# Recurrent branch of a two-layer hybrid block: units of two heads, operands of the next unit beside the chunk chain, modulation moved to attention

## Chip, core and metric

The kernel runs on one core of one Trainium2 chip. The metric is the device time of one execution in microseconds; less is better. TensorE (PE) multiplies, PEld is its loading of weights, VectorE (DVE), ScalarE (ACT) and GpSimd (POOL) do the rest of the arithmetic, and SyncE (SP) issues most of the transfers between memory and the core. All engines run their own instructions in order and wait for each other by semaphores.

## What is computed

Two layers run over 256 latent tokens and 256 context tokens of width 1024. Each layer has an adaptive modulation of the norm, one wide input projection, three branches (latent attention, neighbourhood attention, a recurrent branch), a gated merge and a feed-forward part, which is dense in layer 0 and a mixture of eight experts in layer 1. Layer 1 needs outputs for the latent tokens alone. The parts that this change is about:

```python
mod = (s_lat @ mod_w[l] + mod_b[l])[:, None, :]          # [6 * 1024] per layer, for x and for ctx
h = rms_norm(x, norm1_g[l]) * (1.0 + sc1) + sh1
m_cq, m_ckv, m_kr, n_q, n_k, n_v, r_z, gates = split_last(h @ w_in[l], IN_SIZES)
...
def rwkv_scan(r, w, k, v, kk, a, s0, reverse):
    def step(S, inp):
        r_t, w_t, k_t, v_t, kk_t, a_t = inp
        sa = jnp.einsum('bhij,bhj->bhi', S, -kk_t)
        S = S * w_t[:, :, None, :] + sa[..., None] * (kk_t * a_t)[:, :, None, :] + v_t[..., None] * k_t[:, :, None, :]
        return S, jnp.einsum('bhij,bhj->bhi', S, r_t)
...
x_mid = x + gt1 * merge_branches(ya, yb, yr, gates, mla_wo[l], na_wo[l], rw_wo[l], w_out[l])
```

The scan runs over eight heads of 64, in both directions, first over the context and then over the latents.

## The kernel before

**Stages.** For each layer: norm, recurrent branch, attention start (keys of the latent attention and the operands of the neighbourhood attention), the two attentions with the merge woven in, the output projection, and then the feed-forward part. Only the recurrent branch and the attention are touched here.

**The projection as filler.** `serve` (L451) is a generator that multiplies the normed input with one tile of 128 columns of `w_in` after the other, 57 tiles per layer. A tile is 24 products of 128x512 (three per 128 rows of depth, since each f32 operand is split in two parts whose products make up the f32 result); in layer 1 the tiles that are needed for the latents alone are 256 wide. Its weights come in by SP (512 KB, tile `wraw`, four buffers), ACT makes the upper part `whi` (L469) and POOL the lower part `wlo` (L470). Tiles that the recurrent branch needs stay in SBUF, the others are written to memory (`spill`, L956). `need` (L497) drives the generator until a tile is there.

**Modulation.** `modulation` (L319) is a second generator: a round is eight steps, each of two loads of 512 KB into `wraw` and four products (L339) that fill four strips of one PSUM bank; the next round's result is used only at the end of the layer or in the next one. `serve` takes one such step after each of its tiles (`next(extra, None)`, L492).

**Recurrent branch.** The recurrence is done in chunks of 64 tokens. `rw_half` (L587) treats four heads (two pairs of heads, a pair fills 128 partitions) in both directions. It makes the operands (decays by a scan, L620, exponentials, scaled keys), then the inverse of a 64x64 triangular matrix for each head, direction and chunk: blocks of 16 by substitution on DVE (L701 to L706), merged to 32 and 64 by many 32x32 products (L719, L735, L739, L763 to L772). Then a chain of eight chunks runs (L876 to L908), each of which needs the state `H` of the one before: PE (L882) to ACT (`rs`, L885) to PE (L892) to DVE and ACT (`uv`, L894, L895) to PE (L847) to DVE (`hst`, L850). `rw_front` of the second half runs in the last chunks of the first. `rw_out` (L918) normalizes and stores the result.

**Order of the work.** `weave` (L1634) takes the steps of the recurrent branch in their order; each yields a number of microseconds, and that much of `serve` is put behind it. The order in which instructions then stand on an engine is made from this by the framework's scheduler. PSUM has eight banks: two for the projection (`mm`), one for modulation (`md`), five for the recurrent branch (`rw`).

## Time and profile before

| | us |
|---|---|
| median of three runs | 2992.24 (2989.56 to 2997.04) |
| the profiled execution | 2989.12 |
| its span, first to last instruction | 2987.4 |
| PE busy | 2815.1 (94%), 19774 products |
| PE's weight loads (PEld) busy | 2168.4 (73%) |
| DVE busy | 1901.3 (64%), 2654 instructions |
| ACT busy | 1621.5 (54%), 2449 instructions |
| POOL busy | 369.9 (12%) |

A busy share is an average over stages. Layer 0 takes until about 1260, its recurrent branch 100 to 550; layer 1's recurrent branch lies between 1270 and 1745, and its attention starts there; the experts follow from about 1960. PE counts as busy also where its clock is granted at half rate, so the granted clock is read beside the busy time. The matrix products on small tiles overlap on the engine, so the busy times of their groups add up to more than the time they take.

### The profile page before, as it was taken

The numbers are of one execution on the slowest core, as the hardware profiler recorded it, in microseconds if no ns is written. First come the engines' busy times: TensorE is split into PE (matmuls) and PEld (weight loads), VectorE is DVE, ScalarE is ACT, GpSimd is POOL, SyncE is SP. The second block draws the span as 40 slices with busy tenths as digits, with TensorE's granted clock in tenths as the row PEclk, the third lists the DMA queues.
The fourth block names the chain that finished last, engine by engine and source line by source line (L and its number), as shares of the span: only waits on it lengthen the run. The fifth ranks groups of instructions, "written<-read, shape, count | busy, mean of one in ns | idle before, by whom it ended". The sixth has DMA issues, their size and how long they took to land. (4 is left out here: it accounts for less than half of the span.)

```text
span 2987.4 us, 48726 instructions
## 1 busy us (share of the span) xinstructions
PE 2815.1 (94%) x19774; PEld 2168.4 (73%) x19774; DVE 1901.3 (64%) x2654; ACT 1621.5 (54%) x2449; POOL 369.9 (12%) x287
## 2 busy tenths in 40 slices
PE   7989979999999999997997979989999999999998
PEld 3566667676777888765766856778878787887876
DVE  4653662527754333267347256779988988888897
ACT  3423423447644332253343436667877777777776
POOL 3221221220010000133233400010000000000000
PEclk9989979999999999998997988989999999999999
DMA  7433311441432333343342333669989999998995
GB/s 273 160 130 103 131 57 61 158 143 57 128 127 80 97 99 104 117 143 110 103 149 95 108 104 109 193 239 361 359 320 363 353 350 342 356 361 335 362 352 205
DMA packets 109016, 582.26 MB, mean 195 GB/s; under 512 B 12912, under 2 KB 26608, under 8 KB 86896
## 3 DMA queue, kind: packets, MB, share of 16 engines
q1 hardware_dynamic: 94640, 557.57, 52.1%
q10 hardware_dynamic: 13632, 19.93, 1.8%
q8 instruction: 157, 2.57, 0.4%
q0 software_dynamic: 512, 1.57, 0.1%
q14 instruction: 75, 0.61, 0.1%
HBM read 554.38 MB, written 24.64 MB: 194 GB/s over the span
## 5 line engine op out<-in xcount | busy, mean ns | idle before, releaser
L314 PE MATMUL pmm<-big,whi 128*128 128x512 f32 (+2 forms) x1392 | 534.4, 385 | 11.1 <-ACT stage L958 3.2
L315 PE MATMUL pmm<-big,whi 128*128 128x512 f32 (+2 forms) x1392 | 517.4, 372 | 7.3 <-DVE big L436 3.6
L316 PE MATMUL pmm<-big,wlo 128*128 128x512 f32 (+2 forms) x1392 | 515.9, 371 | 1.9 <-POOL wlo L470 1.9
L1552 DVE TENSOR_TENSOR mwlo<-share,mwhi 128x1024 fp32r<-128x1024 f32 x398 | 472.2, 1229 | 21.0 <-ACT mwhi L1551 11.7
L1551 ACT ACTIVATE mwhi<-share 128x1024 fp32r<-128x1024 f32 x404 | 423.8, 1059 | 94.2 <-PE pmm L316 68.2
L470 POOL TENSOR_TENSOR wlo<-wraw,whi 128x512 fp32r<-128x512 f32 (+1 forms) x228 | 305.0, 1341 | 721.5 <-ACT whi L469 691.9
L315 PE MATMUL pmm<-mwlo,big 128*128 128x512 f32 x896 | 355.1, 396 | 7.2 <-DVE mwlo L1552 6.7
L314 PEld LDWEIGHTS pmm<-big,whi 128*128 128x128 f32 (+1 forms) x1392 | 267.4, 192 | 117.5 <-issue 37.5
L314 PE MATMUL pmm<-mwhi,big 128*128 128x512 f32 x896 | 352.1, 393 | 0.6 <-ACT big L1439 0.6
L316 PE MATMUL pmm<-mwhi,big 128*128 128x512 f32 x896 | 349.8, 390 | 0.0
L299 DVE TENSOR_TENSOR wlo<-wraw,whi 128x512 fp32r<-128x512 f32 x236 | 158.7, 674 | 252.1 <-ACT whi L298 245.6
L1552 DVE TENSOR_TENSOR mwlo<-mraw,mwhi 128x1024 fp32r<-128x1024 f32 x264 | 310.9, 1223 | 9.1 <-ACT mwhi L1551 3.5
L1551 ACT ACTIVATE mwhi<-mraw 128x1024 fp32r<-128x1024 f32 x264 | 278.0, 1060 | 66.8 <-PE pmm L316 49.8
L315 PEld LDWEIGHTS pmm<-big,whi 128*128 128x128 f32 (+1 forms) x1392 | 267.9, 192 | 55.1 <-DVE big L436 6.0
L316 PEld LDWEIGHTS pmm<-big,wlo 128*128 128x128 f32 (+1 forms) x1392 | 268.1, 193 | 50.6 <-issue 5.1
L298 ACT ACTIVATE whi<-wraw 128x512 fp32r<-128x512 f32 x236 | 145.3, 617 | 288.4 <-PE pmm L315 271.9
L469 ACT ACTIVATE whi<-wraw 128x512 fp32r<-128x512 f32 (+1 forms) x228 | 141.8, 624 | 267.4 <-PE pmm L315 228.3
L315 PEld LDWEIGHTS pmm<-mwlo,big 128*128 128x128 f32 x896 | 168.3, 188 | 48.0 <-DVE mwlo L1552 12.3
L314 PEld LDWEIGHTS pmm<-mwhi,big 128*128 128x128 f32 x896 | 168.3, 188 | 36.3 <-ACT big L1439 1.3
L316 PEld LDWEIGHTS pmm<-mwhi,big 128*128 128x128 f32 x896 | 168.3, 188 | 33.4
L315 PE MATMUL pat<-mwlo,mhh 128*128 128x512 f32 x448 | 175.1, 391 | 1.6 <-DVE mwlo L1552 1.4
L314 PE MATMUL pat<-mwhi,mhh 128*128 128x512 f32 x448 | 174.4, 389 | 0.0
(407 smaller groups left out, 4487.0 us busy)
## 6 DMA issues: line engine op xcount, KB each, us to landing
share<-in_moe SPq DMA_DIRECT2D x100, 2048.0 KB, 9.4
mraw<-in_moe SPq DMA_DIRECT2D x66, 2048.0 KB, 9.5
wraw<-in_win SPq DMA_DIRECT2D x112, 512.0 KB, 3.5
wraw<-in_modw SPq DMA_DIRECT2D x80, 512.0 KB, 4.9
wraw<-in_ffn SPq DMA_DIRECT2D x60, 512.0 KB, 3.5
wraw<-in_wo SPq DMA_DIRECT2D x24, 512.0 KB, 3.8
wraw<-in_wout SPq DMA_DIRECT2D x16, 512.0 KB, 4.6
share<-in_modw SPq DMA_DIRECT2D x12, 512.0 KB, 9.0
```

The costliest lines, as they stand in the source:

```text
L298: nc.scalar.activation(hi, raw[:, a:a + b], AF.Copy)
L299: nc.vector.tensor_tensor(lo, raw[:, a:a + b], hi.bitcast(F32), OP.subtract)
L314: nc.tensor.matmul(out, a[0], b[0], start=first, stop=False)
L315: nc.tensor.matmul(out, a[0], b[1], start=False, stop=False)
L316: nc.tensor.matmul(out, a[1], b[0], start=False, stop=last)
L469: nc.scalar.activation(hi, raw[:, k:k + 4], AF.Copy)
L470: nc.gpsimd.tensor_tensor(lo, raw[:, k:k + 4], hi.bitcast(F32), OP.subtract)
L1551: nc.scalar.activation(hi, raw[:, a:a + 2], AF.Copy)
L1552: (nc.gpsimd if a in pool else nc.vector).tensor_tensor(lo, raw[:, a:a + 2], hi.bitcast(F32), OP.subtract)
```

## The change

- **Units of two heads.** `rw_half` becomes `rw_prep` (operands and inverses of one pair of heads) and `rw_chain` (its eight chunks and its output). The chain of pair n runs beside the preparation of pair n+1. The chain has four PSUM banks of its own (`ch`), preparation two (`rw`); each chunk of a pair has half as many products, and copies half as wide.
- **Pacing.** A new function `pace` replaces `weave` there. It keeps a clock for each of the two streams, takes the next step of the one that is behind, adds up an estimate of PE's work, and puts in projection steps while PE's sum is behind the clocks. Steps now yield two numbers, their own time and PE's.
- **Operands.** The scale of the decay and of `kd` moves from DVE to ACT; the backward scan runs on reversed views in place of two corrections; the norm of the keys is made on 128x16 in place of 64x512; the substitution holds two 16-blocks in the partitions' rows as one 16x16 block per item; both `uv` copies are on DVE; `lora` is loaded once.
- **Modulation.** `serve` no longer takes modulation steps. The rounds 1 and 2 of layer 0 and round 0 of layer 1 (24 steps) now alternate with what is left of the projection in layer 0's attention start, the rounds 1 and 2 of layer 1 (16 steps) in layer 1's, and what is left over runs beside the attentions. `router_begin` moves behind them.
- **Rest of the projection.** After the recurrent branch the projection runs until the four `nq` tiles are stored, some of it is woven into the attention start, and all that is left is then done in one piece.

```diff
-    def serve(s, l, t0, extra):
+    def serve(s, l, t0):
...
-            next(extra, None)
             q, q1 = q1, q2
-        for _ in extra:
-            yield 1.0
...
-                V.tensor_scalar(lw, lw, -0.5 * DEC, -0.5 * DEC, op0=OP.mult, op1=OP.add)
-                cum = s.tmp()
-                V.tensor_tensor_scan(cum, s.c("scanm"), lw, 0.0, OP.mult, OP.add)
-                if d:
-                    V.tensor_tensor(lw, lw, cum, OP.subtract)
-                    V.tensor_tensor(c8(lw), c8(lw), c8(cum)[:, :, 63:64].to_broadcast([128, 8, 64]), OP.add)
-                    cum = lw
+            A.activation(lw, lw, AF.Identity, bias=s.m16[:, 98:99], scale=-0.5 * DEC)
...
+            rev = (lambda a: a[:, ::-1]) if d else (lambda a: a)
+            V.tensor_tensor_scan(rev(cum), s.c("scanm"), rev(lw), 0.0, OP.mult, OP.add)
...
+            A.activation(kd, ta, AF.Identity, bias=s.kc1[l][:, hp:hp + 1], scale=s.kc2[l][:, hp:hp + 1])
...
+        for t in range(2, 16):
+            w = pr[:, 0:t * t].rearrange("p (j q) -> p j q", j=t)
+            V.tensor_tensor(w, X[:, t:t + 1, 0:t].to_broadcast([128, t, t]), X[:, 0:t, 0:t].rearrange("p q j -> p j q"), OP.mult)
+            V.tensor_reduce(X[:, t, 0:t], w, AX.X, OP.add)
+            yield 0.4 + t * t / 500.0, 0.0
...
+            yield s.W["chain"], 1.2
+            pu = s.ps(tag="ch")
+            for hh, d in heads:
+                PE.matmul(pu[bp(n, d), col(hh)], TT[HO[d], 8 * hh + ch[d], :], Rs[HO[d], col(hh)], start=(hh == 0), stop=(hh == 1),
+                          skip_group_check=True)
+            for d in range(2):
+                V.tensor_copy(st["uv"][d][bp(n, d)].rearrange("p a b -> p (a b)"), pu[bp(n, d), 0:128])
+            yield s.W["chain"], 0.4
...
+def pace(K, streams, fill):
...
+    while clock:
+        g = min(clock, key=clock.get)
+        w = next(g, None)
...
+        clock[g] += w[0] * K.W["time"]
+        pe += w[1] + K.debt
+        K.debt = 0.0
+        now = min(clock.values())
+        while pe < now:
+            t = next(fill, None)
+            pe += 1e9 if t is None else t
...
         def rwkv(l, t0):
             K.rw_common(l)
...
+            before = []
+            for hp in range(4):
+                K.mark(f"rw{l}{hp}")
+                pace(K, before + [K.rw_prep(l, hp, t0)], K.srv)
+                before = [K.rw_chain(l, hp, t0)]
+            K.mark(f"rw{l}4")
+            pace(K, before, K.srv)
...
-                K.srv = K.serve(l, t0, K.modulation(1, [1, 2]) if l else chain(K.modgen, K.modulation(1, [0])))
-                with K.phase(f"n1{l}", **({} if l else dict(st=1))):
+                K.srv = K.serve(l, t0)
+                mods = K.modulation(1, [1, 2]) if l else chain(K.modgen, K.modulation(1, [0]))
+                with K.phase(f"n1{l}", **({} if l else dict(st=1, md=1))):
...
-                with K.phase(f"rw{l}", rw=5):
...
-                    weave(rwkv(l, t0), K.srv, False)
...
+                with K.phase(f"rw{l}", rw=2, ch=4):
+                    K.W = dict(chain=1.9, time=(1.1, 1.0)[l])
+                    rwkv(l, t0)
+                    while not all((l, f"nq{i}") in K.spilled for i in range(4)):
+                        next(K.srv)
+                with K.phase(f"at{l}", md=1, sc=2, tp=2, py=1):
...
-                    weave(alternate(K.mla_keys(l), K.na_prep(l, t0)), chain(K.srv, mods))
+                    weave(alternate(K.mla_keys(l), K.na_prep(l, t0)), alternate(K.srv, mods), False)
+                    for _ in K.srv:
+                        pass
```

How the order changes on PE inside a chunk of layer 0's first chain. Before, a chunk has the products of four heads (`prw`, L789 scores, L836 and L840 the state), and then projection products (`pmm`):

```order
L789 MATMUL prw_2093<-big_127_719,share_32_289 128x128
L789 MATMUL prw_2094<-big_127_719,share_32_289 128x128
L836 MATMUL prw_2103<-hst_2024,cst 64x256 x2
L840 MATMUL prw_2103<-hst_2024,big_127_719 64x128 x4
L314 MATMUL pmm_2073<-big_30_230,whi_1986 128x512
L315 MATMUL pmm_2073<-big_31_231,whi_1986 128x512
L316 MATMUL pmm_2073<-big_30_230,wlo_1987 128x512
```

In the changed kernel, the second chunk of the first pair. `pch` are products of the chain, L618 and L622 those of the next pair's operands (`prw`), in one order:

```order
L618 MATMUL prw_1331<-zl_337,lora_298 128x512
L867 MATMUL pch_1255<-uv_1205,am_1215 64x64
L867 MATMUL pch_1255<-uv_1206,am_1215 64x64
L867 MATMUL pch_1255<-uv_1205,am_1217 64x64
L867 MATMUL pch_1255<-uv_1206,am_1217 64x64
L622 MATMUL prw_1335<-zl_377,lora_298 128x512
L824 MATMUL pch_1308<-share_34_291,am_1291 64x64 x2
L890 MATMUL pch_1308<-hst_1289,big_42_305 64x128 x2
L803 MATMUL pch_1321<-big_42_305,share_32_289 128x128 x2
L847 MATMUL pch_1326<-hst_1289,cst 64x128 x2
L850 MATMUL pch_1326<-hst_1289,big_42_305 64x128 x2
L900 MATMUL pch_1347<-rs_1318,share_33_290 64x64 x4
```

What moved: where three to six projection products stood between two steps of a chain, products of the next pair's operands now stand, and few projection products. Per layer the three stretches with both streams hold 96, 141 and 96 projection products in layer 0.

SP's queue before, in layer 0's recurrent branch: a projection tile's weights (`in_win`), then one modulation step's two loads (`in_modw`).

```order
L460 DMA wraw_2812<-in_win 128x1024
L334 DMA wraw_2936<-in_modw 128x1024
L334 DMA wraw_2938<-in_modw 128x1024
L460 DMA wraw_2944<-in_win 128x1024
L334 DMA wraw_3053<-in_modw 128x1024
L334 DMA wraw_3055<-in_modw 128x1024
L460 DMA wraw_3061<-in_win 128x1024
```

SP's queue of the changed kernel at the attention start of layer 0:

```order
L334 DMA wraw_5248<-in_modw 128x1024
L334 DMA wraw_5250<-in_modw 128x1024
L334 DMA wraw_5277<-in_modw 128x1024
L334 DMA wraw_5279<-in_modw 128x1024
L334 DMA wraw_5288<-in_modw 128x1024
L334 DMA wraw_5290<-in_modw 128x1024
L460 DMA wraw_5328<-in_win 128x1024
```

What moved: the loads of modulation, one step to a tile before, stand in the attention start eight steps to a tile; 20 of the 24 steps are issued ahead of the piece in which all remaining tiles follow each other.

PE at the same place, the broadcast of the heads' norms (L1139 before, L1142 in the changed kernel). Before:

```order
L1139 MATMUL ptp_5590<-sq_5564,cst 128x512
L1139 MATMUL ptp_5603<-sq_5564,cst 128x512
L315 MATMUL pmm_5576<-big_31_231,whi_5577 128x512
L316 MATMUL pmm_5576<-big_30_230,wlo_5578 128x512
L1139 MATMUL ptp_5609<-sq_5564,cst 128x512
L314 MATMUL pmm_5576<-big_30_230,whi_5577 128x512
L315 MATMUL pmm_5576<-big_31_231,whi_5577 128x512
L316 MATMUL pmm_5576<-big_30_230,wlo_5578 128x512
L1139 MATMUL ptp_5615<-sq_5564,cst 128x512
```

In the changed kernel, with the modulation's products (`pmd`, L339) between them:

```order
L339 MATMUL pmd_5338<-wraw_5370,sT 32x512 x2
L339 MATMUL pmd_5338<-wraw_5372,sT 32x512 x2
L1142 MATMUL ptp_5529<-sq_5481,cst 128x512
L1142 MATMUL ptp_5535<-sq_5481,cst 128x512
L339 MATMUL pmd_5338<-wraw_5381,sT 32x512 x2
L1142 MATMUL ptp_5548<-sq_5481,cst 128x512
L1142 MATMUL ptp_5554<-sq_5481,cst 128x512
L339 MATMUL pmd_5338<-wraw_5383,sT 32x512 x2
L314 MATMUL pmm_5512<-big_30_230,whi_5423 128x512
L1142 MATMUL ptp_5565<-sq_5481,cst 128x512
L339 MATMUL pmd_5338<-wraw_5415,sT 32x512 x2
```

What moved: the attention's own products now stand behind products that wait for a load each. Between the last output of the recurrent branch and the long piece of projection, PE has 126 projection products, 88 of modulation, 48 of the keys' projection (`psc`) and 72 transposes and broadcasts in layer 0; in layer 1 these are 146, 32, 48 and 72.

## Rows read from the trace of the kernel before

**Rows 1.** Busy time by stretch: us, then each engine, granted clock, DMA share, GB/s.
```profile
100.00:220.00 120.00, 107.04 (x1454) 67.46 (x1454) 75.75 (x114) 39.26 (x69) 28.34 (x22) 0.89 0.41 136
220.00:330.00 110.00, 110.00 (x1125) 77.07 (x1118) 36.84 (x63) 38.54 (x78) 20.44 (x16) 1.00 0.35 120
330.00:450.00 120.00, 97.71 (x1446) 72.18 (x1444) 81.90 (x117) 37.39 (x67) 29.74 (x23) 0.83 0.24 82
450.00:540.00 90.00, 90.00 (x954) 67.97 (x954) 25.40 (x43) 33.47 (x68) 18.47 (x14) 1.00 0.26 87
540.00:670.00 130.00, 123.17 (x555) 90.42 (x554) 56.05 (x91) 61.36 (x112) 37.53 (x30) 0.97 0.44 145
1260.00:1430.00 170.00, 146.12 (x1651) 103.84 (x1652) 105.61 (x164) 73.19 (x129) 59.69 (x44) 0.90 0.37 121
1540.00:1650.00 110.00, 87.14 (x1394) 71.83 (x1393) 77.72 (x113) 39.84 (x75) 40.87 (x30) 0.78 0.32 105
1735.00:1825.00 90.00, 70.42 (x297) 43.49 (x293) 55.18 (x119) 40.31 (x78) 1.42 (x3) 0.70 0.24 78
```

**Rows 2.** Waits of PE, 100 to 570: waiter <- releaser: us, times, longest.
```profile
PE prw L662 <- DVE t L660: 16.2, 4, 6.7
...
PE pmd L339 <- DMA wraw<-in_modw: 0.3, 1, 0.3
```

**Rows 3.** Waits of PE, 1260 to 1825.
```profile
PE prw L719 <- DVE share L709: 14.2, 2, 8.7
```

**Rows 4.** Groups of instructions on DVE, 95 to 560: count | busy us, mean ns | idle before.
```profile
L798 DVE TENSOR_TENSOR am<-prw,cst 128x512 f32<-128x512 f32 x32 | 20.7, 685 | 46.4 <-PE prw L789 46.4
L703 DVE TENSOR_TENSOR share<-share 128x8 f32<-128x8 f32 (+13 forms) x28 | 19.7, 704 | 1.0
...
L705 DVE TENSOR_REDUCE share<-share 128x4 f32<-128x8 f32 (+13 forms) x28 | 9.5, 338 | 1.0
...
L894 DVE COPY uv<-prw 64x256 f32<-64x256 f32 x16 | 6.8, 422 | 31.4 <-PE prw L892 29.4 <-ACT whi L469 2.0
...
L622 DVE TENSOR_TENSOR t<-t,t 128x512 f32<-128x512 f32 x4 | 4.6, 1156 | 0.1
L618 DVE TENSOR_SCALAR t<-t 128x512 f32<-128x512 f32 x8 | 4.5, 560 | 7.7 <-ACT t L612 7.7
...
L623 DVE TENSOR_TENSOR t<-t,t 128x512 f32<-128x512 f32 x4 | 3.7, 935 | 0.1
...
L650 DVE TENSOR_SCALAR t<-t,kc,kc 128x512 f32<-128x512 f32 x4 | 3.1, 776 | 0.0
```

**Rows 5.** Groups on PE, 455 to 535, projection and chain.
```profile
L314 PE MATMUL pmm<-big,whi 128*128 128x512 f32 x49 | 21.6, 441 | 0.0
...
L892 PE MATMUL prw<-rs,share 64*64 64x64 f32 x112 | 4.8, 224 | 0.0
```

**Rows 6.** Timeline of PE in a projection tile: start, us, instruction.
```profile
537.12 0.39 PE L314 MATMUL pmm<-big,whi 128*128 128x512 f32 x1
537.35 0.39 PE L315 MATMUL pmm<-big,whi 128*128 128x512 f32 x1
```

**Rows 7.** Busy time by stretch: products of the inverses and of their merge.
```profile
150.00:160.00 10.00, 6.58 (x153) 4.66 (x154) 6.33 (x9) 0.94 (x3) 1.33 (x1) 0.78 0.39 126
190.00:200.00 10.00, 7.97 (x383) 6.70 (x373) 2.69 (x4) 1.65 (x3) 1.89 (x2) 0.84 0.03 8
```

**Rows 8.** Groups on PE, 1645 to 1735: projections 256 wide.
```profile
L314 PE MATMUL pmm<-big,whi 128*128 128x256 f32 x113 | 34.7, 307 | 0.0
```

**Rows 9.** Timeline: two modulation steps, eight products, on PE.
```profile
262.37 1.06 PE L339 MATMUL pmd<-wraw,sT 128*32 128x512 f32 x8
```

**Rows 10.** The page, part 2: GB/s in 40 slices of 74.7 us.
```profile
GB/s 273 160 130 103 131 57 61 158 143 57 128 127 80 97 99 104 117 143 110 103 149 95 108 104 109 193 239 361 359 320 363 353 350 342 356 361 335 362 352 205
```

**Rows 11.** The page, part 6, DMA issues: count, KB each, median us to landing.
```profile
wraw<-in_win SPq DMA_DIRECT2D x112, 512.0 KB, 3.5
wraw<-in_modw SPq DMA_DIRECT2D x80, 512.0 KB, 4.9
```

More of the change, by code (lines that the diff above doesn't have):

```diff
@@ L568, in rw_front @@
[L568 to L569 removed]
+        rt = s.t([128, 16], "rt", 2)
+        A.activation(rt, st[:, 0:16], AF.Sqrt)
+        V.tensor_scalar(rt, rt, 1e-12, None, op0=OP.max)
+        V.reciprocal(rt, rt)
+        yield 4.0, 1.0
         for i in range(2):
             p = s.ps(tag="rw")
[L572 to L574 removed]
@@ new lines, in rw_front, with rw_values @@
+            for tt in range(4):
+                o = 8 * i + 2 * tt
+                for hh in range(2):
+                    PE.matmul(p[64 * hh:64 * hh + 64, 128 * tt:128 * tt + 128], rt[:, o + hh:o + hh + 1].to_broadcast([128, 64]), s.id,
+                              start=(tt == 0), stop=True, skip_group_check=True)
+            V.tensor_tensor(kk[i], kk[i], p, OP.mult)
+        yield 2.0, 1.7
+        s.K = k, kk
+    def rw_values(s, hp, v):
+        PE = s.nc.tensor
+        VN = s.piece(2, 1024 * (hp // 2) + 512 * (hp % 2), 4, 128)
+        p = s.ps(tag="rw")
+        for tt in range(4):
+            PE.transpose(p[:, tt * 128:tt * 128 + 128], v[:, tt * 128:tt * 128 + 128], s.id)
+        s.nc.scalar.activation(VN.rearrange("p a b -> p (a b)"), p, AF.Copy)
+        return VN
@@ new lines, in rw_prep @@
+            V.tensor_tensor(both[:, :, hh].rearrange("p a (c r) -> p a c r", c=8), pc[:, 1].unsqueeze(1).to_broadcast([128, 2, 8, 32]),
+                            m16.unsqueeze(2).to_broadcast([128, 2, 8, 32]), OP.mult)
+            for d in range(2):
+                sl = slice(64 * d + 32, 64 * d + 64)
+                A.activation(AO[sl, 8 * hh:8 * hh + 8, :], pc[sl, 0], AF.Copy)
+            yield 1.5, 1.4
+        Z = s.piece(1, 3584, 16, 32)
+        V.transpose(Z.rearrange("p c (a i) -> p c a i", a=2), AD.rearrange("p i (a c) -> p c a i", a=2))
@@ new lines, in rw_prep @@
+        V.tensor_tensor(F, p.rearrange("p (i c) -> p i c", c=32), s.m16[:, 64:96].unsqueeze(1).to_broadcast([128, 16, 32]), OP.add)
+        yield 2.0, 1.3
+        TT = s.piece(1, 1024 * i, 16, 64)
+        G.memset(TT[32:64, :, 0:32], 0.0)
+        G.memset(TT[64:96, :, 32:64], 0.0)
+        NT = s.t([128, 16, 32], "nt", 1)
+        pt, pn = s.ps(tag="rw"), s.ps(tag="rw")
+        for q in range(16):
+            o = slice(32 * q, 32 * q + 32)
+            for g in range(4):
+                sl = slice(32 * g, 32 * g + 32)
+                PE.matmul(pt[sl, o], (F if g > 1 else XM)[sl, q, :], (XM if g > 1 else F)[sl, q, :], start=(q == 0),
+                          stop=(q == 15), skip_group_check=True)
@@ L777, in rw_half @@
-        Y = s.piece(2, 1024 * old, 4, 256)
+                PE.matmul(pn[sl, o], (XM if g else F)[sl, q, :], (F if g else XM)[sl, q, :], start=(q == 0), stop=(q == 15),
+                          skip_group_check=True)
+        for g in range(4):
+            sl = slice(32 * g, 32 * g + 32)
+            src, dst = pt[sl].rearrange("p (i c) -> p i c", c=32), TT[sl, :, 32 * (g % 2):32 * (g % 2) + 32]
+            if g % 2:
+                V.tensor_copy(dst, src)
+            else:
+                A.activation(dst, src, AF.Copy)
@@ new lines, in rw_prep @@
+        for g in (0, 3):
+            sl = slice(32 * g, 32 * g + 32)
+            src, dst = pn[sl].rearrange("p (i c) -> p i c", c=32), NT[sl]
+            if g:
+                V.tensor_copy(dst, src)
+            else:
+                A.activation(dst, src, AF.Copy)
+        yield 3.5, 2.2
+        W = s.piece(1, 3072, 16, 32)
+        p = s.ps(tag="rw")
+        for q in range(16):
+            o = slice(32 * q, 32 * q + 32)
+            PE.matmul(p[0:32, o], AO[32:64, q, :], TT[32:64, q, 32:64], start=(q == 0), stop=(q == 15), skip_group_check=True)
+            PE.matmul(p[64:96, o], AO[96:128, q, :], NT[96:128, q, :], start=(q == 0), stop=(q == 15), skip_group_check=True)
@@ L1643, in weave @@
         pass
+def pace(K, streams, fill):
+    clock = {g: 0.0 for g in streams}
+    pe = 0.0
+    while clock:
+        g = min(clock, key=clock.get)
+        w = next(g, None)
+        if w is None:
+            del clock[g]
+            continue
+        clock[g] += w[0] * K.W["time"]
[5 more added lines that the diff above has]
+            pe += 1e9 if t is None else t
+        if now < pe - 3.0 < 1e6:
+            for g in clock:
+                clock[g] += pe - 3.0 - now
 def body(tc, I, O, dbg=None, marks=None):
```

486 lines of the change are left out of this document (201 added, 285 removed).

## The prediction

> **What bounds the kernel now.** I looked first at the page's shares: PE is busy for 94% of the span, so at most the rest, and what the clock withholds, can be won unless PE's own work shrinks. By the order of instructions it does not: it lists 136 matrix products more, under 1%, and the small ones of the inverses are as many as before. The gain must therefore come out of stretches where PE idles or runs below full clock. To find those I cut the two recurrent branches and attention starts into stretches [rows 1]. In each row the reader is to add PE's idle time (length less PE's busy time) and its busy time times (1 − granted clock). I call that the loss. Layer 0: 13.0 + 11.8 in 100 to 220 (operands and inverses of the first half), nothing in 220 to 330 (its chain) and in 450 to 540 (the second chain), 22.3 + 16.6 in 330 to 450 (second half's operands), 6.8 + 3.7 in the attention start; 74 in all. Layer 1: 23.9 + 14.6, 22.9 + 19.2 and 19.6 + 21.1; 121 in all. So chains, with the projection as filler, lose nothing, and preparation and attention start lose everything: **195 us** is the ceiling.
>
> Next I asked what ends PE's waits. In layer 0 the longest group is the operands' products waiting for DVE, 16.2 us [rows 2]; in layer 1 the merge waiting for the end of the substitution, 14.2 [rows 3]. Modulation, whose loads come one step to a tile, costs 0.3 us of waiting [rows 2]: it is hidden now.
>
> **The change part by part.** The sum is made against the profiled execution, 2989.1, which lies 3.1 below the median of the runs shown.
>
> *DVE, which sets the preparation.* Layer 0's four pairs take 75.8 + 36.8 + 81.9 + 25.4 us of DVE [rows 1], 55 each, and about 56.5 with the second output. What halving widths costs is seen in two rows: 256 columns 422 ns, 512 columns 685 [rows 4], so 128 more columns cost 132 and some 159 ns are paid per instruction. Masks: 64 at 0.42 for 32 at 0.685, +6. Copies of `uv`: all 64 are now on DVE, 128 wide, 159 + 132 = 0.29 each, 18.6 for 6.8, +12. Substitution: the items are the same, but its 28 row pairs become 56, 56 more instructions at 0.159, +9. Other halved rows (state, transposes, statistics), +8 by the order's counts at the same fixed part. Removed or moved to ACT: 4.6 + 4.5 + 3.7 + 3.1 [rows 4] and some 4 (estimated) of the norm on 64x512, −20. So +15 per layer and **60 per pair**. Spread by the steps in each stretch: 59, 67, 63 in layer 0's three stretches with two streams, 58, 63, 60 in layer 1's. ACT takes the moved steps at no cost: it is busy 38 of 110 to 120 us [rows 1].
>
> The Trainium skill speaks against this part: VectorE: DVE Perf Modes, "Rules for kernel authors", asks to minimize the count of operations, and its errata section puts a fixed part of about 150 cycles on each. By the order DVE has 338 rows more; at that page's 0.156 us (150 cycles at 0.96 GHz) they would cost an estimated 53 us over both layers before what is removed, DVE would need about 63 per pair, and the sum would be near 2984. The trace's 159 ns agrees with the fixed part; where the sums part is in what I credit for the removed wide rows.
>
> *PE in a stretch with two streams.* In 455 to 535 PE runs seven chunks of four heads and 149 projection products: one line has 49 [rows 5], three lines alike. They start 0.23 us apart [rows 6], so 80 − 34 = 46 us are the chain's, 6.5 a chunk, and 3.25 for a pair; eight make 26. The preparation: 448 small products at 7.97 / 383 = 0.021 and 64 of the scores at 6.58 / 153 = 0.043 [rows 7], and four operand products of 0.23: 13. Filler in layer 0 is 96, 141 and 96 products, 22, 33, 22. So PE has **61, 72, 61** of work. In layer 1 a product 256 wide takes (90 − 8 × 6.5) / 339 = 0.11 [rows 8] (113 on that line, three alike), and PE has **57, 53, 51**.
>
> *Both together.* How closely DVE can be packed with two streams no row shows. Bounds: 63% and 68% in the stretches of preparation alone [rows 1], and 100%. I take 90%, nearer the top, because DVE's waits there are for its own stream, and a second stream now stands ready. Stretches then take 66, 74, 70 and 64, 70, 67. Loss: 5 + 2 + 9, **about 15**, in layer 0 and 7 + 17 + 16 = **40** in layer 1. The clock: 0.83 and 0.78 where PE had idled [rows 1]; PE is denser here, so I take **6** per layer, between 0 and the 16.6 and 19.2 of those rows. The first pair's preparation still runs alone: half of the 24.8, **12**; in layer 1 an estimated 8 of the 38.5 for the norm ahead and half of the rest, **23**. The last chain runs beside filler, as in 450 to 540: **0**.
>
> *Modulation in layer 0's attention start.* 20 steps, 40 loads of 512 KB, are issued there ahead of the long piece, and SP's queue carries the projection's weights behind them. PE's work there: 126 and 48 products at 0.235, 88 of modulation at 1.06 / 8 [rows 9], and some 15 us (estimated) of transposes and broadcasts: 69. Loads bound it so: at the best rate of the whole kernel, 363 GB/s [rows 10], 21 MB take 58 us, and nothing is lost; one after the other at 3.5 us each [rows 11], 140 us, and 71 are lost. I take 4.9 per step of two [rows 11], since two or three of the four `wraw` buffers are free for it: 100 us, **31** lost. Queued behind the products that wait for a load are attention's transposes and broadcasts on PE, and behind these DVE. The trace says hidden now (0.3), and that is gone, because the cover, a tile of 24 products per step, is gone.
>
> The Trainium skill has the same under DMA: Bandwidth & Descriptors, "Rules for kernel authors": issue early, compute, and wait late. By that rule a step whose load is issued just ahead of its product shows its whole latency; no row of the kernel before has such a step.
>
> *Layer 1's attention start.* The 40.7 lost there get 146 half-width products (17 us) and 32 of modulation (4): 20 are left if all of that fits, 41 if none; I take **28**. For the 16 moved steps I add **9**: 0 if they are as hidden as now, 25 at layer 0's 31 per 20 steps; the DMA share of 0.24 there [rows 1] leaves room. In the recurrent branches SP's queue loses the modulation's loads; as these cost 0.3, nothing is gained.
>
> Sum: layer 0, 12 + 15 + 6 + 31 = 64 for 74; layer 1, 23 + 40 + 6 + 28 + 9 = 106 for 121. The gain is 25: **2964 us**.
>
> **Rivals.** *DVE binds (slower).* Two streams wait for each other on one in-order DVE: a chain's `uv` copy stands behind a substitution row pair, the chain's next product on PE behind that. For it: the chain's idle time on DVE is all waiting for PE, 46 us before the masks and 29 before `uv` [rows 4]; against it: those waits are what the other stream can fill. At 85% the losses grow to 28 and 52, which uses up the 25; that is the point from which it decides. At 80%: 43 and 65, **3017**.
>
> *Loads bind (no change).* A step's buffers come free only behind its products and the next is issued then: 4.9 + 1.06 = 6 per step, 120 us, 51 lost in place of 31: **2984**. For it: two buffers; against: the steps overlap by pairs when three are free.
>
> *PE binds throughout.* DVE is packed to 95% (losses 6 and 29), and both attention starts lose 20, with nothing for the 16 steps: 12 + 6 + 6 + 20 and 23 + 29 + 6 + 20, 122 lost, **2916**. For it: PE with filler loses nothing in the chains [rows 1]. Against it: six stretches where DVE's sum is already near or above PE's.
>
> That the streams do not interleave at all can be left aside: the order shows the next pair's operands between the chain's products.
>
> **How the numbers follow.** A difference under 0.3%, 9 us, can't be told from none here. My forecast 0.42, DVE binds 0.27, loads bind 0.12, PE binds 0.19. Of the forecast's 0.42 (2944 to 2984, DVE from 87 to 93%) some 0.38 is faster by more than 9; of the loads' case 0.10 lies within 9; nearly all of PE's case is faster; of DVE's case a little is within. This gives faster 0.57, same 0.14, slower 0.29. The range goes from 2912 to 3017: it leaves out the lower tail of PE's case and, above 3017, DVE packed below 80%; at 63 to 68% that would be 3120. The forecast's own range is 2944 to 2984.
>
> **What would show it.** Right: in the stretches with two streams DVE is 85 to 95% busy, PE's waits for operands and substitution shrink to a few us, the granted clock stays above 0.9; the stretches are 64 to 74 us. In layer 0's attention start PE's waits on `wraw` loads appear, some 30 us. Wrong: DVE under 80% busy there with PE waiting for `uv`, masks or substitution; or no wait on loads; or an attention start above 110 us in layer 0.

## The result: slower by 0.7%, and the profile after

The changed kernel takes **3013.07 us** (median of four runs, 3010.42 to 3015.38) against 2992.52 before: a ratio of **1.0067**, 95% interval 1.0050 to 1.0084. The forecast was 2964. The time lies inside the range, near its upper end, but on the other side of no change. The profiled execution took 3010.94 us. Its page, part 1:

```profile
span 3009.2 us, 49850 instructions
...
PE 2884.0 (96%) x20046; PEld 2192.0 (73%) x20046; DVE 1890.5 (63%) x2992; ACT 1668.5 (55%) x2629; POOL 362.2 (12%) x295
```

PE was busy for 2815 us and is now for 2884, although the span grew by 22 only. So PE idles less, as forecast, and is busy for 69 us more with nearly the same products. (The pages count records, 19774 before and 20046 now, and not products: a small f32 product stands as two records, so the 272 more are the 136 products of the prediction.) That is the contradiction to explain.

The stretches of the changed kernel, as in [rows 1]. In order: the first pair's preparation, the three stretches with two streams, the last chain and the attention start of layer 0; then the three stretches with two streams and the attention start of layer 1.

```profile
67.00:133.00 66.00, 60.41 (x815) 43.05 (x814) 44.19 (x85) 31.93 (x56) 19.31 (x15) 1.00 0.20 65
133.00:207.00 74.00, 70.92 (x1107) 49.97 (x1105) 50.34 (x118) 34.43 (x79) 13.25 (x10) 0.98 0.13 44
207.00:296.00 89.00, 85.43 (x1130) 59.10 (x1129) 58.65 (x134) 38.50 (x85) 17.06 (x15) 1.00 0.12 40
296.00:383.00 87.00, 84.09 (x1174) 57.96 (x1174) 55.76 (x129) 38.27 (x84) 11.06 (x9) 0.90 0.12 40
383.00:453.00 70.00, 70.00 (x575) 47.91 (x574) 20.58 (x56) 22.13 (x57) 17.22 (x14) 1.00 0.32 111
453.00:580.00 127.00, 114.73 (x462) 52.48 (x460) 46.22 (x88) 37.58 (x71) 11.66 (x10) 0.93 0.68 229
1392.00:1459.00 67.00, 63.88 (x1061) 47.98 (x1060) 44.60 (x112) 33.22 (x76) 11.93 (x11) 0.95 0.15 49
1459.00:1527.00 68.00, 67.08 (x808) 49.19 (x808) 48.11 (x124) 33.31 (x75) 14.74 (x14) 1.00 0.15 44
1527.00:1602.00 75.00, 69.11 (x1247) 47.77 (x1233) 49.05 (x124) 34.36 (x76) 9.47 (x8) 0.96 0.10 32
1669.00:1746.00 77.00, 70.30 (x333) 41.30 (x332) 35.79 (x65) 30.04 (x55) 13.72 (x12) 0.87 0.57 200
```

The reader is to see two things. In the stretches with two streams DVE is busy for 68, 66, 64, 67, 71 and 65% and not for 90%, so it has slack; and the granted clock there, 0.90 to 1.00, is above the 0.83 and 0.78 of the second halves' preparations in [rows 1] and no lower than the first halves' 0.89 and 0.90. The waits agree. PE over 67 to 453, and below it over the attention start, where [rows 2] had 16.2 us for the operands and 0.3 for a modulation load:

```profile
PE prw L744 <- issue: 4.3, 5, 2.1
PE prw L731 <- DVE share L722: 2.7, 3, 1.6
...
PE pch L867 <- DVE hst L859: 2.0, 4, 0.7
```

```profile
PE psc L314 <- ACT whi L298: 6.8, 2, 3.9
PE pmd L339 <- DMA wraw<-in_modw: 4.1, 3, 3.2
```

**Where PE's time went.** For this table I took every PE record from its start to the start of the next one, less idle time, times the granted clock, and summed by what the product is for. Layer 0 goes from 24 us to the norm ahead of its feed-forward, layer 1 from its first norm to the norm ahead of the experts. What lies behind takes the same time in all these kernels.

| us, layer 0 / layer 1 | chain and preparation | modulation | projection, merge | attention | idle | low clock | length |
|---|---|---|---|---|---|---|---|
| before | 150.0 / 136.5 | 40.2 / 18.7 | 464.1 / 305.7 | 130.3 / 99.7 | 53.1 / 68.9 | 34.3 / 54.9 | 872 / 684 |
| changed | 181.4 / 169.1 | 49.6 / 27.1 | 471.9 / 316.2 | 133.1 / 101.3 | 38.1 / 37.5 | 22.2 / 31.2 | 896 / 682 |
| only modulation moved | 148.8 / 135.3 | 50.4 / 29.1 | 460.3 / 302.8 | 131.9 / 99.7 | 60.6 / 71.3 | 52.5 / 64.2 | 904 / 702 |
| streams apart | 170.1 / 157.3 | 50.6 / 28.1 | 475.8 / 312.5 | 136.0 / 99.2 | 65.4 / 83.2 | 24.5 / 75.9 | 922 / 756 |
| chain held together | 174.2 / 159.9 | 50.4 / 27.1 | 469.1 / 315.4 | 133.2 / 100.3 | 43.1 / 36.0 | 24.5 / 40.1 | 894 / 679 |
| modulation in service | 179.2 / 171.6 | 47.1 / 24.3 | 473.3 / 317.2 | 130.7 / 97.2 | 22.5 / 43.4 | 6.0 / 45.5 | 859 / 699 |
| mixed, all held | 175.7 / 161.7 | 40.0 / 22.5 | 472.6 / 315.3 | 130.6 / 99.2 | 22.6 / 39.4 | 11.8 / 29.3 | 855 / 667 |

Idle time and low clock fell from 211 to 129 us, **82 won**. PE's own work at full clock grew by **104**: 64 in chain and preparation, 18 in modulation, 18 in the projection, 4 in the attention. The difference is the 22 us that the span grew by.

**Why the same products take longer.** A group of the chain's scores before, timeline of PE; each product stands as two records, so x16 is eight products, four heads in two directions:

```profile
236.75 1.16 PE L789 MATMUL prw<-big,share 64*128 64x128 f32 x16
```

In the changed kernel, in the same view: a whole group of one pair, then a group that is cut in two by projection products, and the first projection products behind its first half:

```profile
234.39 0.72 PE L803 MATMUL pch<-big,share 64*128 64x128 f32 x8
...
240.21 0.71 PE L803 MATMUL pch<-big,share 64*128 64x128 f32 x4
240.85 0.50 PE L316 MATMUL pmm<-big,wlo 128*128 128x512 f32 x1
241.18 0.39 PE L314 MATMUL pmm<-big,whi 128*128 128x512 f32 x1
241.41 0.40 PE L315 MATMUL pmm<-big,whi 128*128 128x512 f32 x1
...
243.75 0.71 PE L803 MATMUL pch<-big,share 64*128 64x128 f32 x4
```

Eight products take 1.16 us, four take 0.72, and **two take 0.71**. In the order printed with the change, the two of a cut group are one head's, in both directions; the other head's two use other rows of the array and add 0.01 us when they stand in the same group. So products that use different parts of the array run together, a group cut in half costs twice, and two groups of four cost more than one of eight. The projection pays too: behind the small products the first two starts are 0.33 us apart (240.85, 241.18), the next 0.23. The Trainium skill has the rule that I did not weigh: TensorEngine Tiling (Array Packing), "Key Properties", says that different tiles work in parallel and that a change of the tiling mode drains the engine. The rows agree with both.

Modulation in layer 0's attention start, same view: a step cut in two by attention's products (its second load landed at 520.31, behind the start of its first half), and a whole step.

```profile
519.80 1.05 PE L339 MATMUL pmd<-wraw,sT 128*32 128x512 f32 x4
520.78 0.64 PE L1036 MATMUL ptp<-cst,N 128*96 128x128 f32 x4
...
521.59 1.05 PE L339 MATMUL pmd<-wraw,sT 128*32 128x512 f32 x4
...
525.19 1.13 PE L339 MATMUL pmd<-wraw,sT 128*32 128x512 f32 x8
```

Eight records, four products, take 1.1 us, and four records take as long. The caption of [rows 9] was wrong: its x8 in 1.06 us is **one** step, recorded twice per product, not two.

### The profile page after: what moved, and what is told of

The parts are those of the page before. It is cut to its first block, busy times and chain, and to the rows that moved or that the text cites. A ratio compares the mean times of both kernels' runs of the same rounds, so it can differ in the third digit from the quotient of the medians.

```text
span 3009.2 us, 49850 instructions
## 1 busy us (share of the span) xinstructions
PE 2884.0 (96%) x20046; PEld 2192.0 (73%) x20046; DVE 1890.5 (63%) x2992; ACT 1668.5 (55%) x2629; POOL 362.2 (12%) x295
## 5 line engine op out<-in xcount | busy, mean ns | idle before, releaser
L470 POOL TENSOR_TENSOR wlo<-wraw,whi 128x512 fp32r<-128x512 f32 (+1 forms) x228 | 296.5, 1305 | 820.1 <-ACT whi L469 777.8
L316 PE MATMUL pat<-mwhi,mhl 128*128 128x512 f32 x448 | 174.5, 390 | 0.0
```

What stands on the lines that cost most here:

```text
L316: nc.tensor.matmul(out, a[1], b[0], start=False, stop=last)
L470: nc.gpsimd.tensor_tensor(lo, raw[:, k:k + 4], hi.bitcast(F32), OP.subtract)
```

## The experiments

Ratios are given against the kernel before, run beside each; the changed kernel stands at 1.0067.

**Only modulation moved.** The kernel before, with this part of the change alone.

```diff
-            next(extra, None)
...
-                    weave(alternate(K.mla_keys(l), K.na_prep(l, t0)), chain(K.srv, mods))
+                    weave(alternate(K.mla_keys(l), K.na_prep(l, t0)), alternate(K.srv, mods), False)
+                    for _ in K.srv:
+                        pass
```

> The kernel before, with only the modulation moved from the projection's tiles to the attention stages, as in the change. Theory A (PE pays for cut groups): a modulation step whose two loads land apart runs as two groups of two products that take about 0.98 us each, where a whole step takes 1.02; of the 40 moved steps most are cut, so PE's work on modulation grows by some 18 us over both layers, and layer 0's attention start loses some 10 more, while layer 1's attention start gets work for some 20 us that it idled: 2995 to 3010 us. Theory B (the slowdown is all in the recurrent branch, modulation is hidden wherever it stands): 2980 to 2993, with the modulation's work on PE as before.

Measured: 3039.94 us, ratio **1.0191** (1.0168 to 1.0213). Both theories named too low a time. Layer by layer, recurrent branch and what follows, before and then with the move:

```profile
24.00:546.00 522.00, 479.00 (x5294) 327.46 (x5288) 261.14 (x408) 180.51 (x335) 121.71 (x94) 0.93 0.37 124
546.00:662.00 116.00, 110.19 (x480) 80.46 (x479) 47.10 (x74) 52.77 (x93) 37.53 (x30) 0.97 0.46 148
1267.00:1746.00 479.00, 428.11 (x5336) 331.12 (x5335) 239.02 (x379) 194.54 (x373) 159.99 (x121) 0.91 0.36 121
1746.00:1951.00 205.00, 187.40 (x1174) 136.00 (x1174) 141.30 (x318) 121.57 (x261) 5.43 (x9) 0.88 0.40 128
```

```profile
24.00:527.00 503.00, 455.32 (x5083) 331.43 (x5083) 258.75 (x395) 177.08 (x329) 123.71 (x93) 0.89 0.24 79
527.00:697.00 170.00, 159.69 (x669) 92.81 (x669) 54.92 (x101) 60.15 (x110) 39.20 (x31) 0.96 0.67 223
1298.00:1767.00 469.00, 415.70 (x5207) 332.71 (x5206) 239.12 (x369) 192.33 (x371) 158.62 (x120) 0.89 0.28 92
1767.00:2000.00 233.00, 215.38 (x1303) 141.14 (x1302) 143.92 (x329) 123.50 (x263) 5.91 (x9) 0.90 0.53 176
```

In layer 0 the recurrent branch gets 19 us shorter (522 to 503) and the attention start 54 longer (116 to 170). In layer 1 it is 10 against 28 (the last stretch 205 to 233). The recurrent branch does not give back what it no longer computes: PE idles and falls to the lower clock there instead (0.93 to 0.89). So modulation had been cheap in the recurrent branch, where it filled PE, and is dear in the attention stages.

**Modulation by strips of a quarter.** One load fills all four strips.

```diff
-                    nc.tensor.matmul(acc[32 * j:32 * j + 32, :], s.sT[:, k, :], ws[j // 2][:, 512 * (j % 2):512 * (j % 2) + 512],
+                        nc.tensor.matmul(acc[32 * j:32 * j + 32, 256 * b:256 * b + 256], s.sT[:, k, :], ws[b][:, 256 * j:256 * j + 256],
```

> The changed kernel, with the products of a modulation step cut along the other way: one load feeds all four strips with 256 columns each, so that no group has to wait for a second load to fill the four strips. Theory A (PE pays for cut groups): a load's four products take some 0.5 us, modulation's work on PE falls from 77 to some 55 to 60 us over both layers, and the time by 10 to 18 us, to 2995 to 3003. Theory B (the loads themselves bind the attention starts): PE only waits longer for each load, 3010 to 3015.

Measured: 3008.57, between the two ranges; ratio 1.0084 (1.0064 to 1.0104), which overlaps that of the changed kernel. PE's work on modulation fell by 20 us as A said (76.7 to 56.9), and the time did not follow: in layer 0 idle time and low clock rose from 60 to 77, idle time by 2 and low clock by 15. The attention start, to be held against the 453 to 580 of the changed kernel, and its wait for modulation's loads, 4.1 us there:

```profile
453.00:580.00 127.00, 111.87 (x635) 59.27 (x633) 46.22 (x84) 36.80 (x70) 14.35 (x12) 0.85 0.68 231
```

```profile
PE pmd L340 <- DMA wraw<-in_modw: 8.0, 7, 2.9
```

PE waits longer for loads, as B said (8.0 us for 4.1), and the granted clock falls more (0.85 for 0.93). Whether the loads or the clock hold the time there, no run tells apart.

**Streams apart.** Each preparation and each chain alone.

```diff
-                pace(K, before + [K.rw_prep(l, hp, t0)], K.srv)
-                before = [K.rw_chain(l, hp, t0)]
+                pace(K, [K.rw_prep(l, hp, t0)], K.srv)
+                pace(K, [K.rw_chain(l, hp, t0)], K.srv)
```

> The changed kernel, but each pair's preparation and then its chain run alone with the projection as filler, never two streams. Units are still of two heads. Theory A1 (the groups of the chain are cut by the other stream's products): the work of chain and preparation on PE at full clock falls from 181 and 169 us in the two layers to about 160 and 148, the rest of the growth over 150 and 137 before being the halved groups. Theory A2 (halving alone costs it): it stays within 6 us of 181 and 169. Theory B (DVE bound the changed kernel): idle time and low clock of the preparations come back, 60 us a layer, and the time is above 3030. By A1 the time is 2975 to 3010, since the lost overlap gives back some idle time.

Measured: 3107.62, ratio 1.0392 (1.0371 to 1.0412). Its page, part 1:

```profile
span 3107.9 us, 49980 instructions
...
PE 2908.8 (94%) x20046; PEld 2207.7 (71%) x20046; DVE 1927.3 (62%) x2992; ACT 1672.6 (54%) x2633; POOL 369.2 (12%) x295
```

Chain and preparation take 170.1 and 157.3: between A1's and A2's numbers. Of the growth of 64, **23** go when the streams stand apart, and **41** stay with units of two heads. By line, the 23 are all in the chain; of the 41, 31 stand in the chain and 10 in the preparation, whose products for the norm of the keys the change rewrote too. So halved groups cost 31 us at most, and a few of the chain's groups are still cut by the projection here. Time missed my range for A1 by far: idle time and low clock rose from 129 to 249 us. The sign of B's price came true, its reason did not, since DVE has slack when the streams run together. So running two streams side by side is worth some 95 us to units of two heads.

**Chain held together.** An order on PE alone, with no wait added: in three groups the later products are issued behind the first.

```diff
+    def glue(s, calls):
+        last = None
+        for f, a, k in calls:
+            if last is None:
+                last = f(*a, **k).ins
+            else:
+                with s.tc.issue_after(last):
+                    last = f(*a, **k).ins
...
-                PE.matmul(ph[HO[hh], col(d)], st["bn"][:, d, HO[hh]], UV[d][:, hh, :], start=(H is None and d == 0), stop=(d == 1),
-                          skip_group_check=True)
+            s.glue([(PE.matmul, (ph[HO[hh], col(d)], st["bn"][:, d, HO[hh]], UV[d][:, hh, :]),
+                     dict(start=(H is None and d == 1), stop=(d == 0), skip_group_check=True)) for d in (1, 0) for hh in range(2)])
```

> The changed kernel, with three groups of the chain (scores, state update, right sides: four products each) held together: the first product of a group is the one whose input comes last, and the other three are issued right behind it. Same products, same units, same streams. Theory A1 (cut groups): scores go from 31 whole groups of 64 to nearly all, each cut one saves 0.64 us and each cut state update 0.25; 8 to 10 us a layer, 2990 to 3003. Theory A2 (halving alone): no change, 3010 to 3016. Theory B (waits of the streams bind): a held group waits for its last input and delays what stands behind it, 3015 to 3040.

Measured: 2994.76, ratio 1.0032 (1.0010 to 1.0054). The median lies in A1's range. Chain and preparation fall by 7.2 and 9.2 us of PE, as A1 said, so A2 falls, and B with it. In time it is 0.35% against the changed kernel, and the two intervals just overlap (1.0054 here, 1.0050 there); in the profiled execution, 3004.33, idle time and low clock take back 15 of the 20 us that PE's work falls by. The mixed kernels below show the gain clear of the noise. Not every group is whole even so: its first product can still be issued alone, ahead of other work, and the three behind it later.

**Modulation back in service.** The changed kernel with the modulation part undone; the preparation has one PSUM bank for it.

```diff
+            next(extra, None)
             q, q1 = q1, q2
...
-                with K.phase(f"rw{l}", rw=2, ch=4):
+                with K.phase(f"rw{l}", rw=1, ch=4):
```

> The changed kernel with the modulation's part undone: a step follows each projection tile again, as in the kernel before; units of two heads, pace and operands stay. Since modulation needs a PSUM bank there, the preparation has one bank and not two. Theory A (the move of modulation is the part that costs: it cost 53 us when made alone): 2955 to 2985, modulation back at 59 us of PE work, the loss in layer 0's attention start below 12. Theory B (the units cost it, by their halved groups): 2995 or more. The lost bank may add 0 to 15 us in both.

Measured: 2985.27, ratio **0.9986** (0.9966 to 1.0007): 0.8% below the changed kernel. That is the upper edge of A, and B, 2995 or more, falls. Modulation came back to 71 us of PE only, not to the 59 of A. The two layers differ. Recurrent branch and what follows to the attentions (layer 0) or to the experts (layer 1), changed and then this run:

```profile
24.00:453.00 429.00, 406.32 (x4947) 280.97 (x4947) 254.61 (x569) 184.04 (x394) 95.77 (x79) 0.96 0.21 72
453.00:689.00 236.00, 223.29 (x942) 142.40 (x940) 56.56 (x100) 76.56 (x139) 62.64 (x49) 0.96 0.60 200
1291.00:1669.00 378.00, 356.33 (x4717) 262.34 (x4717) 222.28 (x534) 176.17 (x379) 87.56 (x72) 0.94 0.20 64
1669.00:1973.00 304.00, 288.62 (x1931) 214.12 (x1929) 152.27 (x328) 163.07 (x341) 69.00 (x57) 0.96 0.59 198
```

```profile
24.00:479.00 455.00, 439.53 (x5168) 280.91 (x5161) 260.27 (x580) 188.22 (x398) 93.90 (x79) 0.98 0.36 123
479.00:649.00 170.00, 167.02 (x742) 128.72 (x741) 47.52 (x74) 71.40 (x124) 64.48 (x49) 1.00 0.45 152
1252.00:1668.00 416.00, 392.01 (x4847) 272.56 (x4848) 229.50 (x537) 176.57 (x381) 89.74 (x73) 0.93 0.29 95
1668.00:1951.00 283.00, 264.04 (x1800) 214.47 (x1799) 154.69 (x326) 161.15 (x340) 69.09 (x57) 0.93 0.49 158
```

Layer 0 gets 26 us longer in the recurrent branch and 66 shorter behind it; up to its end it is 37 shorter (896 and 859 in the table). Nearly all of that is idle time and low clock, and only half of it comes from the attention start: in the recurrent branch they fall from 37 to 21 us, behind it from 20 to 3. So the move cost twice, at the place that modulation came to and at the place that it left. Layer 1 gets 38 longer and only 21 shorter. Whether the single bank or the modulation makes those 38, no run tells apart.

**Modulation by tile.** Kept in the attention stages, out of the attention start.

```diff
-                    weave(alternate(K.mla_keys(l), K.na_prep(l, t0)), alternate(K.srv, mods), False)
-                    for _ in K.srv:
-                        pass
+                    weave(alternate(K.mla_keys(l), K.na_prep(l, t0)), K.srv, False)
+                    for n, _ in enumerate(K.srv):
+                        if n % 8 == 7:
+                            next(mods, None)
```

> The changed kernel with the modulation kept in the attention stages but taken out of the attention start: there the projection alone fills, and in the piece of remaining projection that follows one step of modulation comes after each tile. Theory A1 (loads bunched in the attention start bind it, at 6 us a step): idle time and low clock of layer 0's attention start fall from 20 to about 10 us, and 15 to 25 us are won: 2988 to 2998. Theory A2 (only the cut steps cost, wherever they stand): the steps stay cut, 3008 to 3015.

Measured: 3003.35, ratio 1.0050 (1.0030 to 1.0070). The time lies between the two theories; against the changed kernel the intervals overlap, so the time decides nothing. In the trace idle time and low clock of layer 0 fall by 14 us (60 to 46), which is A1's mechanism; PE's work on modulation stays as it was.

**By tile, all held together.** The same with `glue` for chain and modulation.

> As the run before, and the four products of each modulation step and of three groups of the chain are held together. Theory A1 with cut groups: 18 us less of chain and up to 18 less of modulation on PE, against the run before 15 to 30 us faster, 2962 to 2985. If held steps wait for their second load, 5 to 10 of it is lost again.

Measured: 2991.70, ratio 0.9998 (0.9979 to 1.0016): 0.5%, 15 us, below the run before, the low end of what was expected of holding groups together, and level with the kernel before. The range named in us was missed, since the run before had missed its own. PE's work fell as expected, by 15 us in chain and preparation and 26 in modulation (79 to 53 over both layers), but idle time and low clock rose by 41 (112 to 153): most of what was saved on PE won no time.

**One `uv` copy on ACT.**

```diff
-            for d in range(2):
-                V.tensor_copy(st["uv"][d][bp(n, d)].rearrange("p a b -> p (a b)"), pu[bp(n, d), 0:128])
+            V.tensor_copy(st["uv"][0][bp(n, 0)].rearrange("p a b -> p (a b)"), pu[bp(n, 0), 0:128])
+            A.activation(st["uv"][1][bp(n, 1)].rearrange("p a b -> p (a b)"), pu[bp(n, 1), 0:128], AF.Copy)
```

> The changed kernel with one of a chunk's two copies of uv on ACT, as before the change: 32 copies of some 0.29 us a layer leave DVE, 3 us of each stretch with two streams. Theory B (DVE binds there): 6 to 15 us faster, 2998 to 3007. Theory A (PE binds, DVE has slack at 66 to 70% busy): no change, 3009 to 3018.

Measured: 3025.50, ratio 1.0109 (1.0073 to 1.0145). DVE lost 15 us of work, ACT's copy is as fast (272 ns for 289), and nothing was won, so DVE does not bind. The median is above both ranges, but the interval overlaps that of the changed kernel, so it is not shown to be slower. In the profiled execution layer 0's recurrent branch is 4 us longer and what follows has 9 us more of low clock; why is open.

**Mixed.** Modulation in service in layer 0 and as changed in layer 1: four runs side by side.

```diff
-                K.srv = K.serve(l, t0)
-                mods = K.modulation(1, [1, 2]) if l else chain(K.modgen, K.modulation(1, [0]))
+                K.srv = K.serve(l, t0) if l else K.serve(l, t0, chain(K.modgen, K.modulation(1, [0])))
+                mods = K.modulation(1, [1, 2]) if l else iter(())
...
-                with K.phase(f"rw{l}", rw=2, ch=4):
+                with K.phase(f"rw{l}", rw=1 + l, ch=4):
```

> The changed kernel with modulation after each projection tile in layer 0 (preparation with one PSUM bank there) and left as changed in layer 1, where the run with modulation in service took 700 us and the changed kernel 682. If the layers add up: layer 0 as in that run, 39 us shorter than in the changed kernel, layer 1 as changed; about 0.990 to 0.994 of the kernel before, 2960 to 2973. If the gain in layer 0 is given back because layer 1 starts with other buffers or transfers: 0.997 or more.

> As the run before, and three groups of the chain held together. If cut groups cost 8 to 10 us of PE a layer here too: 6 to 15 us below it, 0.986 to 0.991 of the kernel before. If PE has slack where the groups are cut: no difference.

> As the run before, and the four products of a modulation step held together: 1.06 us for a step in place of some 1.4 in layer 0's recurrent branch, 24 steps, up to 9 us less PE work there; 0.983 to 0.990. If the held products wait for the second load: no difference or up to 5 us more.

> As the second of these runs (chain held together), and the modulation's products cut so that each load feeds all four strips. In layer 0, away from the crowded attention start, the saved 0.3 us a step is won: 3 to 8 us below it. In layer 1's attention start the loads bind and nothing is won. If it is no faster, PE's work on modulation is not what that stretch waits for.

| run | us | ratio to before | interval |
|---|---|---|---|
| mixed | 2972.65 | 0.9943 | 0.9926 to 0.9961 |
| and chain held together | 2957.52 | 0.9893 | 0.9872 to 0.9913 |
| and modulation held together | 2952.89 | **0.9882** | 0.9856 to 0.9908 |
| chain held, modulation by strips | 2962.14 | 0.9920 | 0.9895 to 0.9945 |

The layers add up: 0.9943 against 1.0067 is 1.2%, some 37 us, which is layer 0's 37. Holding the chain together gives 0.5% more, as expected and clear of the noise. Holding modulation's steps together is within the interval, and strips win nothing here either, although PE's work on modulation in layer 0's recurrent branch falls from 46.9 to 38.6 us: the clock and the idle time take it back (20 to 29 us). The 3 to 8 us expected of them were missed. The third kernel is faster than the kernel before and than the changed one. Its stretches, layer 0's recurrent branch, attention start with the rest of the projection, attentions, then layer 1's branch and what follows to the experts:

```profile
24.00:471.00 447.00, 429.95 (x5153) 276.88 (x5146) 256.49 (x577) 187.98 (x399) 94.40 (x79) 0.98 0.37 126
471.00:645.00 174.00, 171.16 (x740) 130.26 (x739) 48.30 (x74) 71.33 (x124) 64.09 (x49) 0.97 0.45 147
1249.00:1617.00 368.00, 347.09 (x4717) 254.78 (x4716) 223.12 (x535) 175.84 (x379) 88.62 (x72) 0.94 0.20 65
1617.00:1916.00 299.00, 280.52 (x1933) 214.70 (x1931) 155.58 (x328) 163.75 (x343) 69.31 (x57) 0.96 0.62 201
```

## Why the prediction was wrong, and where it was right

The step that failed stands in its first paragraph: *"The gain must therefore come out of stretches where PE idles or runs below full clock"*, since PE's own work does not shrink. I counted products (136 more) and took their time as fixed. The chain's 46 us for seven chunks of four heads I halved to 3.25 for a pair, and a projection product stayed at 0.23. In layer 0's three stretches with two streams, chain and preparation took 43, 45 and 48 us of PE where the sum has 39 for each, and the same 96, 141 and 96 projection products took 26, 40 and 27 where it has 22, 33 and 22. Over both layers PE's own work grew by 104 us, a term that the sum put at nothing; that is the step that turned the sign. Against the forecast, by stretch, in us:

| stretch | DVE, forecast | DVE | PE's work, forecast | PE's work | length, forecast | length |
|---|---|---|---|---|---|---|
| layer 0, first | 59 | 50.3 | 61 | 69.2 | 66 | 74 |
| second | 67 | 58.7 | 72 | 85.0 | 74 | 89 |
| third | 63 | 55.8 | 61 | 75.9 | 70 | 87 |
| layer 1, first | 58 | 44.6 | 57 | 60.3 | 64 | 67 |
| second | 63 | 48.1 | 53 | 67.1 | 70 | 68 |
| third | 60 | 49.1 | 51 | 67.0 | 67 | 75 |

- **DVE.** The prices were right. Groups on DVE, 60 to 460, answering to [rows 4]:

```profile
L812 DVE TENSOR_TENSOR am<-pch,cst 128x256 f32<-128x256 f32 x64 | 25.2, 417 | 23.5 <-PE pch L803 22.5 <-PE pch L867 0.8
L712 DVE TENSOR_TENSOR xp<-xs 128x4 f32<-128x4 f32 (+13 forms) x56 | 22.5, 401 | 1.4
L903 DVE COPY uv<-pch 64x128 f32<-64x128 f32 x64 | 18.4, 288 | 20.7 <-PE pch L900 18.3 <-ACT whi L469 1.2
L713 DVE TENSOR_REDUCE xs<-xp 128x2 f32<-128x4 f32 (+13 forms) x56 | 13.6, 243 | 1.5
```

  256 columns at 417 ns and 128 at 288 again leave 159 ns per instruction; masks and copies cost 25.2 and 18.4 us where 27 and 18.6 were said. From 24 us to the attentions of layer 0 DVE has 311 us for 308, where I said +15. The priced rows give 4 of the 12: the masks came to +4.5 for +6, the substitution to +7 for +9. Where the other 8 are, in the removed work or in the halved rows, is not worked out here. The spread over stretches was off by some 10 each, because the first preparation took 44 and the last chain 21. The 90% packing was the wrong question: PE fills the stretches first. The sum near 2984 by the page VectorE: DVE Perf Modes of the Trainium skill rests on a DVE that binds, so it falls with it, though the fixed part per instruction agrees.
- **The preparation on PE.** Part of its miss was in the rows already: [rows 7] price a record, and the 64 products of the scores are 128 records, 5.5 us and not 2.8, so that the 13 us should have been 16. (The 448 small ones are records, 224 products, and were priced rightly.)
- **The losses.** First preparation: 12 forecast, 5.6 measured; in layer 1, with the norm, 23 and 23. Stretches with two streams: 21 and 46 with the clock, 19 and 15. Last chain: 0 in both layers, 0 and 2 measured. Here the forecast was too dark, by some 36 us. That the total came within 2% owes much to this error, which made up for part of the other.
- **Modulation.** Forecast: 88 products at 1.06 / 8, 12 us of PE, and 31 us lost on loads. Measured: 36 us of PE at full clock and 20 lost. The first number came from reading one step as two, and a cut step doubles it again. The wait for loads shows as 4.1 us on modulation and 6.8 on the keys' weights behind it. That *"the cover, a tile of 24 products per step, is gone"* was right, and the whole move costs 37 us in layer 0 where its terms came to 21 (31 for the 10 of now). What the terms left out is the recurrent branch, from which modulation was taken at no price ("as these cost 0.3, nothing is gained"): its idle time and low clock are 37 us with the move and 21 without.
- **Layer 1's attention start.** 28 + 9 forecast, 16 measured in the start itself; layer 1 as a whole gained 2 us and not 15, because its PE work grew by 53.
- **The rivals.** "DVE binds" gave 3017, 4 us from the measured time, and was wrong in its mechanism: DVE has a third of the time free, and taking work from it won nothing. "PE binds throughout" had the right engine but priced it with PE's work unchanged. "Loads bind", at 6 us per step, has the length of the attention start right: 20 steps in the 122 us from 455 to 577, where I took 4.9 for a step from [rows 11]. Its mechanism is not shown, since PE's own work was 104 us of them and the waits for modulation's loads 4.
- **The signs.** Of the signs of being wrong, an attention start above 110 us came true (124, from 453 to 577), and DVE was under 80%; but PE did not wait for it, a case that the list did not have.

So the slowdown is two things, each shown by undoing it: modulation's place in layer 0 (37 us there) and cut groups in the chain (0.35% in the changed kernel, 0.5% in the mixed one). Without both, the rest of the change (units of two heads, operands, layer 1's modulation) is worth 1.1%. The 41 us that stay in chain and preparation with units of two heads remain in every such version; that up to 31 of them are halved groups is read from the timeline, and no run undid it.

## What to carry to other kernels

A product's cost on PE is that of its group: before a chain of small products is split in units or woven with another stream, read from the timeline what a whole, a half and a cut group take, and hold groups together in the order. Where a loaded side job fills an engine in one stage, moving it to a stage that already has more transfers than cover pays for it twice. Compare busy time with the work done, not with the span: a busier engine was the bad news here.

## What was not expected of the hardware

Half of a group of tiled products took as long as the whole: 0.71 us for two products and 0.72 for four of the scores, 1.05 for two and 1.06 to 1.13 for four of modulation. And where transfers were dense, less work on PE won no time: with 14 us less of modulation work in layer 0 by strips (49.6 to 35.7), idle time and low clock took 17 back, 15 of them as a lower granted clock. Held groups beside modulation by tile saved PE 41 us in chain, preparation and modulation, and idle time and low clock took as much.
